# Layer 2's input products in the fixed order of steps, with the latents in seven products of halves

## The chip, the cores and the metric

The kernel runs on one core of a Trainium2 chip. That core has a matrix engine (TensorE, PE in the profile; its weight loads are listed as PEld), a vector engine (VectorE, DVE), an activation engine (ScalarE, ACT), a general engine (GpSimd, POOL) and a synchronisation engine (SyncE, SP) which here only issues DMAs. Each works through a queue of its own, in order, and the engines wait for each other by semaphores. The metric is the device time of the whole kernel in microseconds (us). Three runs of the kernel before took 2256.12, 2256.44 and 2257.72 us; the median is 2256.44.

## What is computed

Two layers on one sequence of 512 tokens of 2048 numbers, everything in fp32. Layer 1 mixes tokens by retention, layer 2 by multi-head latent attention (MLA). Both take an input that is normalised and then shifted and scaled by a vector of modulation, and both multiply their result by a gate.

```python
def mla_branch(h, pos, w_in, q_norm_g, w_uq, kv_norm_g, w_ukv, w_out):
    proj = h @ w_in
    cq, ckv, k_rope, g = jnp.split(
        proj, [MLA_Q_RANK, MLA_Q_RANK + MLA_KV_RANK, MLA_Q_RANK + MLA_KV_RANK + MLA_ROPE], axis=-1)
    q = (rmsnorm(cq, q_norm_g) @ w_uq).reshape(B, S, MLA_HEADS, MLA_NOPE + MLA_ROPE)
    q = jnp.concatenate([q[..., :MLA_NOPE], rope(q[..., MLA_NOPE:], pos)], axis=-1)
    kv = (rmsnorm(ckv, kv_norm_g) @ w_ukv).reshape(B, S, MLA_HEADS, MLA_NOPE + MLA_V)
    k_rope = rope(k_rope[:, :, None, :], pos)
    ...
    return (jax.nn.silu(g) * o) @ w_out

def reference(...):
    c_act = jax.nn.silu(c)
    for i in range(DEPTH):
        mod = (c_act @ ada_w[i] + ada_b[i])[:, None, :]
        shift, scale, gate = jnp.split(mod, 3, axis=-1)
        h = rmsnorm(x, norm_g[i]) * (1.0 + scale) + shift
        ...
        x = x + gate * y
    return rmsnorm(x, final_norm_g)
```

The latents cq and ckv have 512 columns each, the rotary key 64, the gate g 2048, so w_in of layer 2 is 2048 x 3136.

## The kernel before

**Products.** TensorE multiplies in fp32r, which holds fewer digits than fp32. Every operand is therefore split into a high part (a cast, on ScalarE) and a low part (the difference, on VectorE): `split`, lines 131 to 133. A product is three matmuls, high by high, low by high and high by low (`mm3`, lines 156 to 160). A tile is 128 x 128 weights against up to 512 columns. Weights come in units, mostly 256 rows by 512 columns (512 KB): a load on SP's queue, a split, and then 2 x 4 products, 24 matmuls.

**Seven products.** Layer 1's value and gate projections don't use 2 x 2 products of halves but seven products of sums and differences of halves (the scheme of Strassen in Winograd's form): `form_sums` (line 593) forms the sums of the activations, `seven_steps` (line 682) loads weights, forms their sums and runs sixteen steps for each head.

**The list of steps.** Layer 1 is a list `steps`, gone through in one loop (lines 1274 to 1314). Each `Step` has units of weights (load, prepare), matmuls, evacuations, and hooks `beside` them. Loads run three units ahead, the preparation (split) one step ahead. In step i the loop issues loads, prepares step i+1, uses modulation that is ready, runs the step's matmuls, does the additions of the modulation rows fetched before, fetches new rows (`rows` of the next step), and evacuates. The wrappers `behind` and `queued` set the place of instructions in the engines' queues when the program is built; afterwards the order is fixed. `n_p` is the step at which layer 1's pool of buffers is changed and the rotary tables are loaded back.

**Modulation rows.** The later pieces of the modulation come beside other work, a row at a time (`later_modulation`, line 811): SP loads 512 KB of ada_w into one of two buffers (`mod_aw`, line 819), VectorE multiplies it by an element of c and adds it to `mod_am` (line 828). After 16 rows TensorE sums the piece over partitions by matmuls with ones (`sum_modulation`, line 834), and `use_modulation` (line 854) stores it. The last two pieces, 32 rows, are layer 2's gate vector.

**The boundary.** At the end of layer 1, token blocks of 128 are finished one after the other. `x1_out` adds the residual and stores x, `x1_token` (line 1237) scales the block by its norm, in place, on ScalarE (line 1241) and VectorE (line 1242). `h2_pair` (line 1209) transposes two column blocks of x for two token blocks on TensorE into a PSUM bank (x1T, line 1217) and turns them into high and low parts of layer 2's input h2 on ScalarE (lines 1230, 1232) and VectorE (lines 1234, 1235). Banks of that kind come from `aux`, banks for accumulation from `acc`.

**Layer 2 before.** After the list, layer 2 runs by `chunk` and `run`: cq, ckv (`low_rank`, line 1425, 8 units of 24 matmuls each), the rotary keys kr (`kr_unit`, 48 matmuls, each weight column twice), and four gate groups g2 of 8 units of 24 matmuls. A modulation row is fetched with each of the 32 gate units (`next_row`, line 1410). The latents' transposes (cqT, ckvT, line 1449) come in the first group. Then follow the up projections uq and ukv, attention and the output projection.

Of the kernel before, what the change touches and what calls it, by code (L numbers as in the profile page):

```python
# [22 lines left out]
RH = 8  # L23
# [26 lines left out]
def hybrid_trunk_kernel(  # L50
# [219 lines left out]
    def rotary_tables(cos, sin, col, signed, name, queue):  # L270
# [3 lines left out]
        r, k, kh = sin, cos, pos_i.bitcast(F32)  # L274
        DVE.tensor_copy(r, pos_i)
# [179 lines left out]
    tables_d = dram.tile([2 * P, T], F32, name="tables_d")  # L455
# [55 lines left out]
    for u in range(NU):  # L511
# [27 lines left out]
        if more:  # L539
            for k in range(4, KD):  # L540
                queued(add_row, am, aw[k // 2], k, False)
        else:
            for _ in range(7):
                queued(next, tables)
# [38 lines left out]
    sums = {}  # L583

    def sums_tile(n):
# [5 lines left out]
        return lpp.tile(shape, F32R, tag="sums", bufs=4, name=f"sums_{n}")  # L591

    def form_sums(u):
        e, o = (tmp(f"h_{2 * u + i}_f") for i in range(2))
        for f, kt in ((e, 2 * u), (o, 2 * u + 1)):
            DVE.tensor_add(f, hT[kt][:, 0, :].bitcast(F32), hT[kt][:, 1, :].bitcast(F32))
        f = lpp.tile([P, 4, H], F32, tag="own_r", bufs=3, name=f"sums_{u}_f")
        DVE.tensor_add(f[:, 0, :], e[:, H:], o[:, H:])
        DVE.tensor_sub(f[:, 1, :], f[:, 0, :], e[:, :H])
        DVE.tensor_sub(f[:, 2, :], e[:, :H], e[:, H:])  # L600
        DVE.tensor_sub(f[:, 3, :], o[:, :H], f[:, 1, :])
        for i in range(2):
            s = sums_tile(2 * u + i)
            split(f[:, 2 * i : 2 * i + 2, :], s[:, :, 0, :], s[:, :, 1, :])
            sums[2 * u + i] = s

    def form(n, u, b):

        if isinstance(n, tuple):
            kt, half = n  # L610
            o = half * H + b * P
            return tuple(hT[2 * u + kt][:, a, o : o + P] for a in range(2))
# [15 lines left out]
    def plain_steps(nu, kn, parts, cn, name, take, n, lhs, rhs, evac, **kw):  # L628
# [3 lines left out]
        def step(u):  # L632
# [13 lines left out]
            def multiply():  # L646
# [6 lines left out]
                for ki, b in order:  # L653
                    last = u == nu - 1 and ki == kn - 1
                    mm3(banks[b], lhs(w["hl"], ki, u * kn + ki, b), rhs(w["hl"], ki, u * kn + ki, b), u + ki == 0, last)
# [6 lines left out]
            return Step(load, prepare, multiply, follow, **{k: v(u) for k, v in kw.items()})  # L662
# [6 lines left out]
    turn = [0, 0]  # L669

    def raw_tile(shape, name):
        turn[0] += 1
        if turn[0] % 2:
            return base.tile(shape, F32, tag="raw", bufs=3, name=f"{name}_r")
        return lpp.tile(shape, F32, tag="own_r", bufs=3, name=f"{name}_r")

    def part_tiles(shape, name):
        turn[1] += 1
        pool, tags, n = (lpp, ("own_h", "own_l"), 1) if turn[1] % 4 == 0 else (base, ("whi", "wlo"), 3)
        return [pool.tile(shape, F32R, tag=tag, bufs=n, name=f"{name}_{tag[-2]}") for tag in tags]  # L680

    def seven_steps(h):
# [3 lines left out]

        def block(kt, j):
            return wvg[kt * P : (kt + 1) * P, j, h * T : (h + 1) * T]
# [13 lines left out]
        def step(second, u):  # L702
# [54 lines left out]
            def follow():  # L757
# [9 lines left out]
                if second and u == KD // 2 - 1:  # L767
                    for b in range(2):
                        keep_rows(x_[b], v_d, h * T + b * P, f"v{h}_st{b}")
                    for b in range(2):  # L770
                        keep_rows(s_[b], g_d, h * T + b * P, f"g{h}_st{b}", AF.Silu, tmp)
                    for b in range(2):
                        r0 = h * T + (2 + b) * P
                        DVE.tensor_add(m4[b], m4[b], y_[b])
                        POOL.dma_start(v_d[r0 : r0 + P, :], m4[b])
                        DVE.tensor_add(m5[b], m5[b], y_[b])
                        ACT.activation(m5[b], m5[b], AF.Silu)
                        POOL.dma_start(g_d[r0 : r0 + P, :], m5[b])
# [16 lines left out]
    for h in range(1, RH):  # L795
# [9 lines left out]
        steps += seven_steps(h)  # L805
# [356 lines left out]
    wide = [o1_unit(3, 0, u, 1, 2 * T, 2 * (("big", 16),) if u in (4, 5) else (("whi", 3), ("wlo", 3))) for u in range(8)]  # L1162
# [9 lines left out]
    for t in range(NT):  # L1172
# [64 lines left out]
    def x1_token(t):  # L1237
        s1 = small(f"x1_s1_{t}")
        DVE.tensor_reduce(out=s1, in_=ss1[t], axis=AX.X, op=ALU.add)
        r = rsqrt(s1, 1, 1.0 / D, f"x1_{t}")  # L1240
        ACT.activation(x1[t][0], x1[t][0], AF.Identity, scale=r)
        DVE.tensor_scalar(out=x1[t][1], in0=x1[t][1], scalar1=r, scalar2=None, op0=ALU.mult)
        if t == 3:
            h2_pair(0, 8, KD)
            h2_pair(1, 0, KD)


    def all_rows():
# [3 lines left out]
        yield from later_modulation(pools["l1"], [(1, 1, n) for n in range(2)], ("odd1", "odd0"))  # L1252

# [20 lines left out]
    for i, step in enumerate(steps):  # L1274
        clock[0] = i
        if i == n_p:
# [3 lines left out]
            with behind(S_):  # L1280
                for n, name in enumerate(("cos", "sin")):
                    rotary.append(rot(pools["l1"], name))
                    nc.sync.dma_start(rotary[n], tables_d[n * P : (n + 1) * P, :])
        with behind(S_):
            while n_loaded < min(n_prepared + 3, len(loads)):
                loads[n_loaded]()
                n_loaded += 1
            for load in step.beside["load"]:
# [14 lines left out]
        with behind(V_, A_):  # L1303
# [3 lines left out]
            if step.sums is not None:  # L1307
                form_sums(step.sums)
# [429 lines left out]
```

## Time and profile before

| | |
|---|---|
| median of three runs | 2256.44 us |
| profiled execution, its own time | 2255.62 us |
| its span (first to last instruction) | 2253.9 us |
| mean granted clock of TensorE | 0.993 |
| layer 2 from the first x1T (1498.38) to the first uq matmul (1799.86) | 301.48 us |
| HBM read, written | 388.59 MB, 42.48 MB |

The profile is one execution, recorded on the chip. A page lists each engine's busy time, the chain of waits that ended last (followed back from the last instruction), the costliest groups of instructions and the DMA issues. A group is given by its line in the kernel, its engine and operation, output <- inputs with the names of the program, tile shapes and count, then busy time in us, mean length of one in ns, and the idle time of that engine just before, with what ended it. A line of a timeline begins with the start and the length in us; in brackets is the idle time before it and its cause. Matmuls overlap: the distance between their starts, not their length, is what one costs.

### The profile page before, as it was taken

How to read it: one execution, taken by the hardware profiler on the slowest of the kernel's cores; microseconds unless marked ns; L12 is line 12 of the kernel's file. 1: busy time of each engine (PE TensorE's matmuls, PEld its weight loads, DVE VectorE, ACT ScalarE, POOL GpSimd, SP SyncE). 2: the span in 40 equal slices, each digit the busy share in tenths (PEclk: the TensorE clock that was granted, in tenths of full speed). 3: DMA queues.
4: the chain of work that ended last, by engine and by line, in shares of the span. 5: the costliest groups of instructions: out<-in, count | busy, mean ns of one | idle time of the engine just before them, and what ended most of it. 6: DMA issues, size and time to landing. Idle time of an engine off the chain costs nothing.

```text
span 2253.9 us, 27801 instructions
## 1 busy us (share of the span) xinstructions
PE 2193.4 (97%) x10198; PEld 1819.2 (81%) x10198; DVE 1528.9 (68%) x2272; ACT 988.6 (44%) x1488; POOL 113.8 (5%) x205
## 2 busy tenths in 40 slices
PE   5999999999999999999999999999999999999997
PEld 4887888888888888878888888878888888888886
DVE  7988867776676789656777767455454367777545
ACT  5664433434343444434445445444322255555433
POOL 1000000100000000000000000010000000000000
PEclk9999999999999999999999999999999999999999
DMA  9974686767767678564655564532466432235433
GB/s 342 347 240 162 197 292 188 265 213 248 239 219 255 217 248 282 196 201 146 209 173 201 168 206 159 188 125 89 133 222 224 152 106 80 85 99 173 150 126 117
DMA packets 236650, 432.94 MB, mean 192 GB/s; under 512 B 21256, under 2 KB 95072, under 8 KB 236512
## 3 DMA queue, kind: packets, MB, share of 16 engines
q1 hardware_dynamic: 223664, 392.49, 53.9%
q0 software_dynamic: 12416, 38.39, 4.3%
q8 instruction: 80, 1.31, 0.2%
q14 instruction: 58, 0.48, 0.1%
q10 hardware_dynamic: 432, 0.27, 0.0%
HBM read 388.59 MB, written 42.48 MB: 191 GB/s over the span
## 4 chain that ended last, share of the span: by engine, by line
PE 76%; issue 10%; DVE 7%; ACT 5%; DMA 1%; POOL 0%; SPq 0%; POOLq 0%; DVEq 0%; ACTq 0%
PE o L1110 12%; PE qk L160 4%; PE qk L159 4%; PE qk L158 4%; PE g L158 3%; PE g L159 3%; PE g L160 3%; PE o L158 2%; PE o L160 2%; PE o L159 2%; PE x L694 2%; PE y L695 2%; PE x L695 2%; PE y L693 2%; PE y L694 2%
## 5 line engine op out<-in xcount | busy, mean ns | idle before, releaser
L1110 PE MATMUL o<-o_whi,o_h 128*128 128x512 f32 x496 | 194.7, 393 | 0.0
L1110 PE MATMUL o<-o_wlo,o_h 128*128 128x512 f32 x496 | 193.7, 391 | 0.0
L1110 PE MATMUL o<-o_whi,o_l 128*128 128x512 f32 x496 | 193.6, 390 | 0.0
L158 PE MATMUL qk<-hT,qk_h 128*128 128x512 f32 x448 | 176.8, 395 | 3.4 <-ACT qk_h L132 3.4
L160 PE MATMUL qk<-hT,qk_l 128*128 128x512 f32 x448 | 176.3, 393 | 1.0 <-DVE qk_l L133 1.0
L159 PE MATMUL qk<-hT,qk_h 128*128 128x512 f32 x448 | 175.4, 392 | 0.0
L828 DVE SCALAR_TENSOR_TENSOR mod_am<-mod_aw,cact,mod_am 128x1024 f32<-128x1024 f32 x120 | 153.5, 1279 | 11.4 <-DMA mod_aw<-in_ada_w_dram 11.0
L133 DVE TENSOR_TENSOR o_wlo<-o_r,o_whi 128x1024 fp32r<-128x1024 f32 x62 | 75.7, 1223 | 87.8 <-ACT o_whi L132 87.7
L1110 PEld LDWEIGHTS o<-o_whi,o_l 128*128 128x128 f32 x496 | 93.5, 189 | 19.6
L133 DVE TENSOR_TENSOR qk_l<-qk_r,qk_h 128x1024 fp32r<-128x1024 f32 x56 | 68.1, 1222 | 60.2 <-ACT qk_h L132 59.7
L1110 PEld LDWEIGHTS o<-o_wlo,o_h 128*128 128x128 f32 x496 | 93.5, 188 | 19.0
L1110 PEld LDWEIGHTS o<-o_whi,o_h 128*128 128x128 f32 x496 | 93.5, 189 | 19.0
L158 PEld LDWEIGHTS qk<-hT,qk_h 128*128 128x128 f32 x448 | 84.9, 189 | 21.7 <-ACT qk_h L132 4.1
L158 PE MATMUL g<-h,g_hi 128*128 128x512 f32 x256 | 100.6, 393 | 1.1 <-ACT ckv_n L1435 1.1
L160 PEld LDWEIGHTS qk<-hT,qk_l 128*128 128x128 f32 x448 | 84.8, 189 | 20.6 <-DVE qk_l L133 3.0
L158 PE MATMUL o<-o_w_hi,o_h 128*128 128x512 f32 x256 | 100.1, 391 | 0.0
L159 PE MATMUL o<-o_w_lo,o_h 128*128 128x512 f32 x256 | 99.8, 390 | 0.0
L159 PE MATMUL g<-h,g_hi 128*128 128x512 f32 x256 | 99.6, 389 | 0.0
L160 PE MATMUL g<-h,g_lo 128*128 128x512 f32 x256 | 99.6, 389 | 0.0
L160 PE MATMUL o<-o_w_hi,o_l 128*128 128x512 f32 x256 | 99.6, 390 | 0.0
L159 PEld LDWEIGHTS qk<-hT,qk_h 128*128 128x128 f32 x448 | 84.8, 189 | 18.1 <-issue 0.5
L132 ACT CAST qk_h<-qk_r 128x1024 fp32r<-128x1024 f32 x56 | 57.9, 1049 | 88.5 <-PE qk L159 63.5
(1358 smaller groups left out, 5763.0 us busy)
## 6 DMA issues: line engine op xcount, KB each, us to landing
mod_aw<-in_ada_w_dram SPq DMA_DIRECT2D x128, 512.0 KB, 5.2
aw<-in_ada_w_dram SPq DMA_DIRECT2D x128, 256.0 KB, 6.0
o_r<-in_ret_w_out_dram SPq DMA_DIRECT2D x64, 512.0 KB, 4.4
qk_r<-in_ret_w_in_dram SPq DMA_DIRECT2D x112, 256.0 KB, 3.9
g_raw<-in_mla_w_in_dram SPq DMA_DIRECT2D x32, 512.0 KB, 3.7
o_w_raw<-in_mla_w_out_dram SPq DMA_DIRECT2D x32, 512.0 KB, 3.7
qk_d<-qk_st POOLq DMA_DIRECT2D x32, 256.0 KB, 3.9
qk_r<-qk_d SPq DMA_DIRECT2D x32, 256.0 KB, 6.2
```

The lines of the kernel that those rows point to most:

```text
L132: ACT.copy(hi, src)
L133: DVE.tensor_sub(lo, src, hi.bitcast(F32))
L158: PE.matmul(o, lhs[0], rhs[0], start=first and not seeded, stop=False, skip_group_check=seeded)
L159: PE.matmul(o, lhs[0], rhs[1], start=False, stop=False, skip_group_check=seeded)
L160: return PE.matmul(o, lhs[1], rhs[0], start=False, stop=last, skip_group_check=seeded)
L693: PE.matmul(banks[b], a[0], w[0], start=first, stop=False, skip_group_check=True)
L694: PE.matmul(banks[b], a[0], w[1], start=False, stop=False, skip_group_check=True)
L695: PE.matmul(banks[b], a[1], w[0], start=False, stop=True, skip_group_check=True)
L828: DVE.scalar_tensor_tensor(out=am, in0=aw, scalar=ck, in1=am, op0=ALU.mult, op1=ALU.add)
L1110: PE.matmul(o, a[i], w[j][:, ki, cols], start=first and i + j == 0, stop=last and i == 1, skip_group_check=True)
```

## The change

1. Layer 2's input products become steps of the list: five steps `front`, the rest of gate group 0 (`ga`), gate group 1 (`g1`), the latents, gate groups 2 and 3 (`g23`). The loop opens layer 2's pool at the first of them (`n_l2`).
2. cq and ckv are computed together by seven products, with the two latents as the two halves of the columns: 16 steps, 336 matmuls of 512 columns in place of 384. `form_sums` forms the sums of h2 beside steps of gate groups 0 and 1.
3. The rotary key's weights lie high and low part side by side in 128 columns. Two passes, with h2's high and low part, make 64 matmuls of 256 columns in place of 48 of 512; then the two halves of the result are added (`kr_sum`) and the rotation follows (`kr_rope`).
4. The first three units of gate group 0 and the rotary keys are multiplied for the first 256 tokens (`ga_half(u, 0)`, `kr_half(0)`), then for the others. The second half of h2 is transposed beside them. In the last token's step, pairs 0 and 1 of the first half are transposed during its matmuls, pairs 2 and 3 before token 3's scaling, pairs 4 to 7 behind it (`last_token`).
5. The rotary tables of MLA are computed beside the last steps of layer 1, stored, and loaded back at `n_l2`.
6. The 32 rows of layer 2's gate vector are fetched in `g23` only: one in each of the first four steps, two in each of the other twelve; what remains is fetched behind the last step.
7. In layer 1, rows are taken in all steps of the second phases from head 5 on (before: head 6), sums of modulation run in the last head's second phase, and at `n_p` the loads of weights stand ahead of those of the tables. One unit of the output projection's weights goes to another buffer.

The core of the diff, with removed parts of layer 2 (`low_rank`, `kr_unit`, the four groups, `next_row`) left out where only their place changes:

```diff
-            return Step(load, prepare, multiply, follow, rows=int(second and (u % 2 == 1 or (h > 5 and u > 0))))
...
+            lambda second, u: int(second and (u % 2 == 1 or (h > 4 and u > 0))),
+            lambda second, u: second and h == RH - 1 and 2 < u < 7,
...
-        step.follow = lambda t=t: (x1_out(0, t), x1_out(1, t), x1_token(t))
+        step.follow = lambda t=t: (x1_out(0, t), x1_out(1, t), x1_scale(t, x1_factor(t)))
...
         if (t, r) == (3, 1):
-            queued(h2_pair, 0, 0, 8)
+            queued(h2_pair, 0, 0, 4)
...
-        if t == 3:
-            h2_pair(0, 8, KD)
-            h2_pair(1, 0, KD)
-
+    def last_token():
+        x1_out(0, 3)
+        x1_out(1, 3)
+        r = x1_factor(3)
+        h2_pair(0, 4, 8)
+        x1_scale(3, r)
+        h2_pair(0, 8, KD)
+
+    steps[-1].follow = last_token
...
+    def ga_half(u, th):
...
+        cols = slice(th * H, (th + 1) * H)
+        hi, lo = ga[u].w["hl"]
+        for ki in range(2):
+            for b in range(4):
+                o = ga[0].banks[b][:, cols]
+                for i, (w, a) in enumerate(((hi, 0), (hi, 1), (lo, 0))):
+                    PE.matmul(
+                        o, w[:, ki, b * P : (b + 1) * P], h2[2 * u + ki][:, a, cols],
+                        start=u + th + ki + i == 0, stop=False, skip_group_check=True,
+                    )
...
+    def kr_half(th):
+        cols = slice(th * H, (th + 1) * H)
+        if th == 0:
+            kr["ps"] = aux("kr_ps")
+        for kt in range(KD):
+            for a in range(2):
+                PE.matmul(
+                    kr["ps"][:, cols], kr["w"][kt // 8][:, kt % 8].rearrange("p j n -> p (j n)"), h2[kt][:, a, cols],
+                    start=kt + a == 0, stop=kt == KD - 1 and a == 1, skip_group_check=True,
+                )
...
+    front[0].multiply = lambda: (ga_half(0, 0), ga_half(1, 0), queued(h2_pair, 1, 0, 4))
+    front[1].multiply = lambda: (ga_half(2, 0), kr_half(0), queued(h2_pair, 1, 4, 8))
+    front[2].multiply = lambda: (ga_half(0, 1), ga_half(1, 1), queued(h2_pair, 1, 8, 12))
+    front[3].multiply = lambda: (ga_half(2, 1), ga[3].multiply(), queued(h2_pair, 1, 12, KD))
+    front[4].multiply = lambda: (ga[4].multiply(), kr_half(1))
+    steps += front + ga[5:]
+    ga[5].beside["form"].append(kr_sum)
+    ga[6].beside["form"].append(kr_rope)
+    g1 = g2_steps(1)
+    steps += g1
...
+    for u, step in enumerate((ga[5], ga[7], g1[0], g1[2], g1[3], g1[5], g1[6], g1[7])):
+        step.beside["form"].append(lambda u=u: form_sums(u, h2, sums2, staged2, more2))
...
+    steps += seven_steps(
+        "c", lambda kt, j: wc[kt * P : (kt + 1) * P, j, :], lambda n, u, b: form(h2, sums2, n, u, b), *turns2,
+        latent_rows, lambda second, u: 0, lambda second, u: False,
+    )
+    g23 = g2_steps(2, rows=lambda u: 1 if u < 4 else 2) + g2_steps(3, rows=lambda u: 2)
+    for i, n, g_c in ((0, "q", qn_c), (1, "kv", kvn_c)):
+        g23[i].beside["form"].append(lambda n=n: latent_norm(n))
+        g23[i + 1].beside["form"].append(lambda n=n: latent_scale(n))
+        g23[2 + 2 * i].beside["multiply"].append(lambda n=n: latent_transposes(n))
+        g23[3 + 2 * i].beside["form"].append(lambda n=n, g_c=g_c: latent_parts(n, g_c))
+    for step in g23[8:]:
+        step.banks_free = True
+    steps += g23
...
+        yield from later_modulation(pools["l2"], [(1, 2, n) for n in range(2)])
...
+        if i == n_l2:
+            assert not ripe and not summed
+            l1.__exit__(None, None, None)
+            l2 = tc.tile_pool(name="l2", bufs=1)
+            pools["l2"] = l2.__enter__()
         with behind(S_):
             while n_loaded < min(n_prepared + 3, len(loads)):
                 loads[n_loaded]()
                 n_loaded += 1
+            if i in (n_p, n_l2):
...
-    assert next(later, None) is None and not fetched and not ripe and not summed
-    l1.__exit__(None, None, None)
+    for adds in (fetched, later):
+        for add in adds:
+            add()
+    sum_modulation(0)
+    use_modulation()
```

More of the change, by code (lines that the diff above doesn't have):

```diff
@@ new lines, in hybrid_trunk_kernel, with next_tables @@
+    steps[-1].follow = last_token
+    mla_tables = []
+    def next_tables():
+        if not mla_tables:
+            pair = [rot(pools["l1"], f"mla_{n}") for n in ("cos", "sin")]
+            mla_tables.extend((rotary_tables(*pair, 1, True, "mla", nc.sync), pair))
+        if next(mla_tables[0], 0) == 0:
+            for n, t in enumerate(mla_tables[1]):
+                POOL.dma_start(tables_d[(2 + n) * P : (3 + n) * P, :], t)
+    for i in range(10):
+        steps[n_p + 65 + i].beside["form"].append(next_tables)
```

341 lines of the change are left out of this document (180 added, 161 removed).

## The prediction

> **What bounds the kernel now.** I read the page first: busy shares, the chain of waits, the costliest groups and the DMA issues.
>
> ```profile
> span 2253.9 us, 27801 instructions
> PE 2193.4 (97%) x10198; PEld 1819.2 (81%) x10198; DVE 1528.9 (68%) x2272; ACT 988.6 (44%) x1488; POOL 113.8 (5%) x205
> PE 76%; issue 10%; DVE 7%; ACT 5%; DMA 1%; POOL 0%; SPq 0%; POOLq 0%; DVEq 0%; ACTq 0%
> L158 PE MATMUL qk<-hT,qk_h 128*128 128x512 f32 x448 | 176.8, 395 | 3.4 <-ACT qk_h L132 3.4
> L160 PE MATMUL qk<-hT,qk_l 128*128 128x512 f32 x448 | 176.3, 393 | 1.0 <-DVE qk_l L133 1.0
> L828 DVE SCALAR_TENSOR_TENSOR mod_am<-mod_aw,cact,mod_am 128x1024 f32<-128x1024 f32 x120 | 153.5, 1279 | 11.4 <-DMA mod_aw<-in_ada_w_dram 11.0
> L158 PE MATMUL g<-h,g_hi 128*128 128x512 f32 x256 | 100.6, 393 | 1.1 <-ACT ckv_n L1435 1.1
> mod_aw<-in_ada_w_dram SPq DMA_DIRECT2D x128, 512.0 KB, 5.2
> ```
>
> TensorE is busy 97% of the span and carries most of the chain, so a matmul less is its issue time less, and a stall of TensorE is a stall of the end. The last two columns of a group show where TensorE still waits: 3.4 and 1.0 us on retention weights, 1.1 us before the first gate group of layer 2.
>
> Then I cut layer 2's stretch before attention into stages. Columns: window, length, busy time and instructions by engine, granted clock, DMA share, GB/s.
>
> ```profile
> 1498.38:1562.80 64.42, 58.68 (x269) 46.16 (x268) 35.93 (x68) 36.56 (x69) 3.35 (x6) 0.95 0.28 85
> 1562.80:1606.50 43.70, 43.70 (x194) 35.96 (x192) 20.54 (x33) 15.28 (x26) 2.48 (x5) 1.00 0.39 117
> 1606.50:1617.38 10.88, 10.88 (x49) 8.96 (x48) 4.46 (x5) 2.71 (x5) 0.92 (x2) 1.00 0.45 147
> 1617.38:1636.81 19.43, 18.37 (x89) 15.24 (x88) 14.11 (x17) 9.74 (x15) 0.55 (x1) 1.00 0.50 151
> 1636.81:1709.29 72.48, 72.48 (x329) 60.31 (x328) 38.56 (x36) 20.21 (x25) 4.05 (x8) 1.00 0.68 219
> 1813.46:1819.21 5.75, 5.75 (x49) 5.74 (x48) 3.35 (x5) 3.19 (x6) 0.00 (x0) 1.00 0.32 94
> ```
>
> The first window is the boundary (layer 1's last token, the transposes of x, then cq), the second ckv, the third the rotary keys, the fourth the transposes of cq and the first three gate units. The key window is 48 matmuls of 512 columns in 10.88 us: 0.2267 us each (their listed 0.39 us overlap). The ckv window gives the same, 192 in 43.70. The last row is 48 matmuls of 256 columns in 5.75 us: 0.120 each, a little over half.
>
> ```profile
> 1498.38 1.47 PE L1217 MATMUL x1T<-ident,x 128*128 128x128 f32 x12
> 1499.61 0.71 PE L1110 MATMUL o<-o_big,o_h 128*128 128x512 f32 x2
> ```
>
> Twelve transposes go out in the 1.23 us between these two rows of TensorE's timeline, 0.10 each. So the boundary's work is 12 output matmuls, 192 of cq and 64 transposes: 2.7 + 43.5 + 6.4 = 52.6 us. It takes 64.42, so about 11.8 us are stall (and slower clock: 0.95 granted).
>
> **The arithmetic.** Latents: 384 matmuls of 512 columns become 336, −48 × 0.2267 = −10.9 us. Keys: 48 × 0.2267 = 10.9 become 64 × 0.120 = 7.7, −3.2. Three gate units on halves: 72 × 0.2267 = 16.3 become 144 × 0.120 = 17.3, +1.0. Sum −13.1 us. All of it is on the path, as TensorE has no other cover.
>
> **Retention weights.** The waits of 3.4 and 1.0 us are one place, the change of pools at layer 1's seventh q/k unit. In the changed order weight loads stand ahead of the rotary-table loads on SP's queue there, and layer 1's modulation rows have been summed earlier. I take −4.4; bounds −4.4 and 0.
>
> **The keys' tail.** In the fourth window 73 matmuls and 16 transposes need 16.5 + 1.6 = 18.1 of 19.43 us. The new order puts the latents' transposes a whole step after their scaling, so −1.3; bounds −1.3 and 0.
>
> **The boundary.** What governs it is ScalarE and VectorE, which turn transposed x into h2 pair by pair:
>
> ```profile
> 1501.67 1.15 ACT L1241 ACTIVATE x<-x,x_r 128x1024 f32<-128x1024 f32 x1 [3.63 <-DMA x_d<-x]
> 1502.73 0.54 ACT L1230 ACTIVATE h<-x1T,b_col,a_col 128x256 fp32r<-128x256 f32 x1
> 1513.42 0.69 DVE L1084 TENSOR_TENSOR x<-o_g,o_xr 128x512 f32<-128x512 f32 x1
> 1519.32 1.15 ACT L1241 ACTIVATE x<-x,x_r 128x1024 f32<-128x1024 f32 x1 [2.17 <-DMA x_d<-x]
> 1524.86 0.61 ACT L1232 ACTIVATE h2f<-x1T,b_col,a_col 128x256 f32<-128x256 f32 x1
> 1526.21 0.63 ACT L1232 ACTIVATE h2f<-x1T,b_col,a_col 128x256 f32<-128x256 f32 x1
> 1510.00:1530.00 20.00, 15.84 (x70) 11.90 (x70) 15.70 (x33) 15.02 (x33) 1.69 (x3) 0.83 0.25 79
> ```
>
> ScalarE takes 1.35 us a pair (1524.86 to 1526.21). Twice it stands in its queue behind the scaling of x, which waits until x has been stored: the last sum on VectorE ends at 1514.11, the scaling starts at 1519.32, 5.2 us later. The units on half the tokens are there so that TensorE can start when tokens 0 and 1 are ready. But queues run in order, and I read the changed order engine by engine. On TensorE all eight transposes of the first half stand ahead of the first half-token matmul, and each from the third on waits for a bank that VectorE and ScalarE have to empty. On VectorE the two sums of token 3, four instructions, stand between pairs 2 and 3, and on ScalarE token 3's scaling, with its wait for the store, stands between pairs 4 and 5. From the first transpose: pair 1 at +4.3 us (1502.73, that wait is unchanged), two pairs to about +7, the four VectorE instructions to +10, the store to +15.1, the scaling 1.15, then pairs 5 to 7 with their VectorE halves to about +22.4. Until then TensorE has 12 output matmuls and 32 transposes, 5.9 us; it idles 16.5, and 0.8 more later, where ScalarE's 11 us for the other half's pairs meet 12.5 us of half-token and key matmuls. That is 17.3 against 11.8: +5.5. Bounds: −10 (the wait for the store alone decides, and every other stall goes) and +8 (the 0.83 clock lasts 15 us longer, 0.17 × 15 on top).
>
> [...]
>
> **Start of the seven products.** Their first accumulations need the banks of gate group 1, which ScalarE must empty, with the split of the first weights in the same queues. In the trace of before no layer-2 row shows it; the gate group's wait of 1.1 us in the page is nearest. The seven-product form opens with two sets of banks instead of one, so I take +2; bounds 0 and 4.
>
> **Work put beside the gate steps.** Eight sums of h2 add on VectorE, by sizes, about 4.4 us each (two of 512 elements, four of 256, two split differences): 35 us; ScalarE's copies less. They lie beside 16 gate steps of 5.44 us. In before's gate window VectorE is busy 38.56 of 72.48 us with a modulation row per unit, and those rows are gone from there, so they cost nothing; uncovered they would cost those 35 us. The tables' stores (POOL) and reloads (SP) are four transfers of 256 KB in low-traffic stretches: nothing.
>
> **The modulation rows.** This is the term that decides. Before, 32 rows of 512 KB are spread over 32 units. After, they come only in gate groups 2 and 3: one a step for four steps, two a step for twelve, four left for after the last step. Each is a load into one of two buffers and a VectorE addition; a load is issued only when its buffer's addition is done. What such a pair takes is in before's trace, in places where two rows came together with a gate load:
>
> ```profile
> 1651.65 2.60 DVE L828 SCALAR_TENSOR_TENSOR mod_am<-mod_aw,cact,mod_am 128x1024 f32<-128x1024 f32 x2
> 1657.62 1.28 DVE L828 SCALAR_TENSOR_TENSOR mod_am<-mod_aw,cact,mod_am 128x1024 f32<-128x1024 f32 x1 [0.44 <-DMA mod_aw<-in_ada_w_dram]
> ...
> 1652.95 1.66 SPq L819 DMA_DIRECT2D mod_aw<-in_ada_w_dram  x2
> ...
> 1740.46 2.60 DVE L828 SCALAR_TENSOR_TENSOR mod_am<-mod_aw,cact,mod_am 128x1024 f32<-128x1024 f32 x2
> 1746.38 1.28 DVE L828 SCALAR_TENSOR_TENSOR mod_am<-mod_aw,cact,mod_am 128x1024 f32<-128x1024 f32 x1 [0.39 <-DMA mod_aw<-in_ada_w_dram]
> ...
> 1653.00:1659.00 6.00, 6.00 (x29) 4.95 (x28) 3.75 (x3) 1.05 (x1) 0.00 (x0) 1.00 0.79 266
> ...
> mod_aw<-in_ada_w_dram SPq DMA_DIRECT2D x28, 512.0 KB, 4.6
> g_raw<-in_mla_w_in_dram SPq DMA_DIRECT2D x27, 512.0 KB, 3.8
> ```
>
> From addition to addition it is 5.97 us (1651.65 to 1657.62), and 5.92 at the second place. It is 1.28 of addition and some 4.65 of load, and VectorE ends up waiting for the DMA. A gate step is 24 × 0.2267 = 5.44 us. So a pair a step does not fit: it runs late by 0.53 us a step, and the four left over have no step at all. Behind a waiting addition stand, in VectorE's queue, the splits of the next weights; in SP's queue, behind a row's load, the loads of gate, uq and ukv weights; in TensorE's queue the two matmuls that sum the last vector stand in the middle of uq, after its first 21 matmuls, with the rest of attention behind.
>
> There are 14 pairs. The first comes in step 5 of the 16, the second stands behind the ckv latents' parts on VectorE, which I place 13.5 us after the start of step 5. From there the rows need 12 × 5.97 + 2.6 + 0.3 = 74.5 us to the last sum. TensorE has left 12 × 5.44 − 13.5 + 16 transposes (1.6) + 21 × 0.2267 (4.8) = 58.2 us. Difference +16.3. Bounds: a load as fast as a gate load (3.8) makes the pair 5.1 us and the term +6; a load of 5.2, the median of all rows in the page, makes it 6.5 and +23.
>
> [...]
>
> **Sum.** −13.1 − 4.4 − 1.3 + 5.5 + 2.0 + 16.3 = +5.0 us on the profiled execution's 2255.62 (its span is 1.7 of that shorter; nothing here changes those): 2260.6. The median of the runs shown is 0.8 above it, 2256.44, so I say 2261; the rivals' times stand on that median too.
>
> **The rivals.**
> 1. Rows keep up (faster). If a row lands like a gate load, 3.8 us, the term is +6 and the sum −5.3: 2251.1; if the boundary's stall does not grow either, −10.8: 2245.6. For: bandwidth is left by the rows above. Against: 5.97 and 5.92 were measured with just these three loads in flight. It decides from a pair of 5.2 us downwards (12 × 5.2 + 2.9 − 58.2 = +7.1, sum −4.2). Chance 0.27; it is the case the bandwidth figure speaks for.
> 2. Traffic piles up (slower). Three loads of 512 KB in each step and the gate stores load the DMA for 65 us without a pause, where before shows 0.79 for 6 us; the pair goes to 6.5 us or over, and the term to +23 and more: sum +11.7, 2268.1. It decides from a load of 5 us upwards. For: the median of 5.2 us over all rows. Against: 4.6 in the gate groups. Chance 0.18.
> 3. No net change. The half-token units fill the boundary as before's cq does, its term is 0, and the sum −0.5: 2255.9. For: the early matmuls exist. Against: they stand behind eight transposes. Chance 0.15.
>
> My forecast keeps 0.40. About 0.2%, 4.5 us, is what a measurement of this kernel tells from no change. The forecast's +5.0 lies just beyond it, so of its 0.40 I give 0.31 to slower and 0.09 to no change; with case 2, slower has 0.49; no change 0.09 + 0.12 from case 3 = 0.21; faster 0.27 + 0.03 = 0.30. The range takes in most of 1, and 2 with the load of 5.2 and 5 us of boundary: 2246 to 2273. The forecast's own is 2257 to 2266.
>
> **What would show it.** In the changed profile: TensorE waiting on DVE for a transpose ahead of the first half-token matmul (boundary), some 17 us between first transpose and there; waits of L160 on weight splits late in gate group 3, and a wait of over 8 us at the last vector's sum inside uq; additions a pair apart by 6 us; the 3.4 us at the retention weights gone. Wrong would be: additions 5.4 us apart or less, no hole in uq, or half-token matmuls within 10 us of the first transpose; or 256-column matmuls far from 0.120 us each.

## The result, and the profile after

| | before | changed |
|---|---|---|
| median | 2255.34 us (22 runs, 2251.9 to 2257.72) | 2251.93 us (22 runs, 2246.94 to 2254.86) |
| profiled execution, span | 2255.62, 2253.9 us | 2254.86, 2253.1 us |

The changed kernel takes 0.9985 of the time of the one before, with a 95% interval of 0.9979 to 0.9992: 3.4 us faster. The forecast was 2261, 5 us slower. The time lies in the range of the prediction, the sign is wrong. The changed kernel's profiled execution is the slowest of its 22 runs, so its profile shows less gain (0.8 us) than the medians.

The page of the changed kernel:

```profile
span 2253.1 us, 28084 instructions
PE 2178.4 (97%) x10238; PEld 1812.8 (80%) x10238; DVE 1601.9 (71%) x2389; ACT 1012.1 (45%) x1526; POOL 113.9 (5%) x201
PE 72%; DVE 12%; DMA 7%; ACT 5%; issue 4%; POOL 0%; SPq 0%; ACTq 0%; DVEq 0%; POOLq 0%
L857 DVE SCALAR_TENSOR_TENSOR mod_am<-mod_aw,cact,mod_am 128x1024 f32<-128x1024 f32 x120 | 153.6, 1280 | 34.9 <-DMA mod_aw<-in_ada_w_dram 34.8
L158 PE MATMUL qk<-hT,qk_h 128*128 128x512 f32 x448 | 175.3, 391 | 0.0
```

TensorE has 15 us less to do, and the wait of 3.4 us at qk is gone. VectorE's waiting for modulation rows has grown from 11.4 to 34.9 us, and the chain that ended last now has 12% of DVE and 7% of DMA, where it had 7% and 1%.

TensorE's waits in the whole of the changed kernel, the main ones (what it waited for; us in total, times, longest):

```profile
PE xT_ps L476 <- ACT x L453: 17.5, 4, 10.5
PE mod_ps L877 <- DVE mod_am L857: 10.7, 1, 10.7
PE x1T L1246 <- DVE h2f L1263: 8.9, 3, 5.7
...
PE uq L160 <- DVE uq_lo L133: 2.4, 1, 2.4
PE x1T L1246 <- DVE o_g L1112: 1.3, 1, 1.3
PE g L160 <- DVE g_l L133: 1.1, 2, 0.6
```

The first is at the start of the program and was 17.3 us before. Of the others the longest are at the two places that the prediction named: the sum of the last modulation vector in uq (10.7 and 2.4 us), and the transposes at the boundary (8.9 and 1.3 us).

The stages of the changed kernel, in the columns used for the kernel before:

```profile
939.00:1000.00 61.00, 61.00 (x278) 50.92 (x277) 32.83 (x42) 21.05 (x28) 6.47 (x12) 1.00 0.69 229
1490.95:1550.84 59.89, 49.66 (x334) 45.12 (x332) 37.34 (x72) 34.16 (x66) 3.37 (x6) 0.89 0.30 95
1550.84:1610.70 59.86, 59.86 (x266) 49.57 (x265) 47.52 (x79) 25.43 (x37) 2.20 (x4) 1.00 0.40 127
1722.00:1780.00 58.00, 57.45 (x249) 46.07 (x248) 37.58 (x34) 14.48 (x20) 5.28 (x10) 1.00 0.79 270
1780.86:1807.44 26.58, 13.48 (x41) 8.99 (x40) 13.89 (x16) 3.88 (x6) 2.08 (x4) 0.68 0.72 241
```

The first is the change of pools in layer 1. The second runs from the first transpose of x to the end of the keys' second half: the boundary. Its work is 12 output matmuls, 64 transposes, 144 + 64 matmuls of 256 columns and 48 of 512: 2.7 + 6.4 + 25.0 + 10.9 = 45.0 us, so 14.9 us are stall. The third, 264 gate matmuls, runs without a gap (264 × 0.2267 = 59.85) although VectorE is busy for 47.52 us of it. The last runs from the first uq to the first uk matmul: 36 matmuls, 8.2 us, and the vector's sums, some 1.3, take 26.58 us.

Layer 2 began at 1490.95 in place of 1498.38 us, 7.4 earlier; its first uk matmul starts at 1807.44, in the kernel before at 1808.02. From the first transpose on, the changed kernel is therefore 6.9 us slower in its profiled execution, 316.49 against 309.64. What it won, it won before layer 2 and in matmuls; what it lost, it lost at the boundary and in uq.

### The profile page after: what moved, and what is told of

Same layout as the page of the kernel before. It is cut to its first block, busy times and chain, and to the rows that moved or that the text cites. A ratio compares the mean times of both kernels' runs of the same rounds, so it can differ in the third digit from the quotient of the medians.

```text
span 2253.1 us, 28084 instructions
## 1 busy us (share of the span) xinstructions
PE 2178.4 (97%) x10238; PEld 1812.8 (80%) x10238; DVE 1601.9 (71%) x2389; ACT 1012.1 (45%) x1526; POOL 113.9 (5%) x201
## 4 chain that ended last, share of the span: by engine, by line
PE 72%; DVE 12%; DMA 7%; ACT 5%; issue 4%; POOL 0%; SPq 0%; ACTq 0%; DVEq 0%; POOLq 0%
PE o L1139 12%; PE qk L160 4%; PE qk L158 4%; PE qk L159 4%; DMA aw<-in_ada_w_dram 2%; DMA mod_aw<-in_ada_w_dram 2%; PE o L158 2%; PE o L160 2%; PE o L159 2%; PE x L696 2%; PE y L696 2%; PE x L697 2%; PE y L697 2%; PE y L695 2%; PE x L695 2%
## 5 line engine op out<-in xcount | busy, mean ns | idle before, releaser
L857 DVE SCALAR_TENSOR_TENSOR mod_am<-mod_aw,cact,mod_am 128x1024 f32<-128x1024 f32 x120 | 153.6, 1280 | 34.9 <-DMA mod_aw<-in_ada_w_dram 34.8
L370 DVE SCALAR_TENSOR_TENSOR am<-aw,cact,am 128x512 f32<-128x512 f32 x118 | 88.7, 752 | 3.6
L160 PE MATMUL g<-h,g_l 128*128 128x512 f32 x232 | 90.6, 391 | 0.6 <-DVE g_l L133 0.6
L158 PE MATMUL g<-h,g_h 128*128 128x512 f32 x232 | 91.0, 392 | 0.0
```

The lines of the kernel that those rows point to most:

```text
L158: PE.matmul(o, lhs[0], rhs[0], start=first and not seeded, stop=False, skip_group_check=seeded)
L160: return PE.matmul(o, lhs[1], rhs[0], start=False, stop=last, skip_group_check=seeded)
L370: DVE.scalar_tensor_tensor(out=am, in0=aw[:, k % 2], scalar=ck, in1=am, op0=ALU.mult, op1=ALU.add)
L857: DVE.scalar_tensor_tensor(out=am, in0=aw, scalar=ck, in1=am, op0=ALU.mult, op1=ALU.add)
```

## The experiments

Times are medians of the runs in question; the ratio is to the kernel before, timed on the same chip. "Against changed" is the difference to 2251.93. The kernel before took 2255.15 to 2255.94 us on these chips (medians), and the intervals reach 2 to 3 us to either side, so a difference of 1 us shows nothing.

| run | what | median us | ratio, 95% interval | against changed |
|---|---|---|---|---|
| e1 | half of the rows go to attention | 2239.44 | 0.9927, 0.9914 to 0.9941 | −12.5 |
| e2 | four row buffers | 2237.27 | 0.9923, 0.9911 to 0.9936 | −14.7 |
| e7 | e2, two rows in every step | 2238.80 | 0.9928, 0.9916 to 0.9940 | −13.1 |
| e5 | latents by plain products | 2262.23 | 1.0028, 1.0016 to 1.0039 | +10.3 |
| e4 | layer 1's edits undone | 2260.25 | 1.0022, 1.0013 to 1.0030 | +8.3 |
| e9 | only the order of loads undone | 2251.65 | 0.9984, 0.9975 to 0.9993 | −0.3 |
| e10 | only the rows and sums undone | 2259.05 | 1.0012, 1.0003 to 1.0021 | +7.1 |
| e8 | no half-token units | 2258.84 | 1.0018, 1.0009 to 1.0027 | +6.9 |
| e3 | half-token units ahead of transposes | 2252.11 | 0.9990, 0.9981 to 0.9999 | +0.2 |
| e12 | token 3's scaling last | 2250.83 | 0.9979, 0.9971 to 0.9988 | −1.1 |
| e13 | e2 and e12 | 2237.34 | 0.9916, 0.9902 to 0.9930 | −14.6 |
| e14 | e2, e12 and e3 | 2240.52 | 0.9932, 0.9918 to 0.9946 | −11.4 |

### The modulation rows: e1, e2, e7

```diff
 e1
-    g23 = g2_steps(2, rows=lambda u: 1 if u < 4 else 2) + g2_steps(3, rows=lambda u: 2)
+    g23 = g2_steps(2, rows=lambda u: 1) + g2_steps(3, rows=lambda u: 1)
...
+            next_row()
             run(uq, 1)
...
             run(uq)
+            next_row()
             next(a0)
             next(a1)
+            next_row()
             run(ukv_chunk(pr + 1, *tiles_[2:]))
```

> The changed kernel with one modulation row in each of the sixteen gate steps instead of two, and the other sixteen rows between the heads of attention. Theory (a pair of rows takes 6.01 us from addition to addition in the changed profile, a gate step 5.44, so the rows end late and TensorE stands 2.4 + 10.7 us in uq and then runs at a lower clock): the hole in uq goes, the first uq to the first uk matmul falls from 26.6 us to about 9, and the whole is 15 to 18 us shorter than the changed kernel, some 2235. Rival (the hole is there for another reason, such as the loads of uq and ukv weights or the splits after a long queue on VectorE): the hole shrinks by less than half and the time stays within 6 us of the changed kernel. Rival two (rows cost the same wherever they lie): attention grows by what uq loses, time as the changed kernel.

The hole is gone. TensorE's timeline, the first uq and the first uk matmul, of e1:

```profile
1778.28 0.39 PE L158 MATMUL uq<-qT,uq_hi 128*128 128x512 f32 x1
...
1786.44 0.39 PE L158 MATMUL uk<-kvT,ukv_hi 128*128 128x512 f32 x1
```

From one to the other it is 8.16 us, which is 36 × 0.2267 with nothing between. From the first transpose to uk it is 295.35 us, 21.1 less than in the changed kernel's profile. In the time only 12.5 us show. Part of the difference is that profile itself, 2.9 us above its median; part is given back: from uk to the end of the span e1 takes 451.3 us, the changed kernel 445.7. The theory held, 2.5 us short of its range; the second rival, that rows cost wherever they lie, holds for some 5.6 us of attention.

```diff
 e2
+                if (i, sect) == (1, 2):
+                    aw = base.tile([P, 2, T], F32, tag="k4b", bufs=4, name=f"{name}_aw{k}")
```

> The changed kernel with four buffers for the modulation rows of layer 2 instead of two; rows are fetched at the same steps and the same bytes move. Theory (the pair's 6 us is waiting for the two buffers: 4.65 us of load after 1.28 us of addition): with loads issued two earlier, rows keep up with the 5.44 us steps, only the four rows left over behind the last step remain, and the time falls by 10 to 15 us against the changed kernel, to about 2238 to 2242. Rival (the DMA's bandwidth, 275 GB/s in this stretch, sets the pair's 6 us): pairs stay 6 us apart, the time within 3 us of the changed kernel.

e2 moves the same bytes in the same steps. It is 14.7 us faster, as the theory had it, so the two buffers were the limit, and not what the DMA can carry in this stretch. The additions in the changed kernel, on VectorE, the second and the last of the pairs, with what they waited for:

```profile
1722.69 2.60 DVE L857 SCALAR_TENSOR_TENSOR mod_am<-mod_aw,cact,mod_am 128x1024 f32<-128x1024 f32 x2
...
1794.78 1.28 DVE L857 SCALAR_TENSOR_TENSOR mod_am<-mod_aw,cact,mod_am 128x1024 f32<-128x1024 f32 x1 [0.26 <-DMA mod_aw<-in_ada_w_dram]
1797.74 1.28 DVE L857 SCALAR_TENSOR_TENSOR mod_am<-mod_aw,cact,mod_am 128x1024 f32<-128x1024 f32 x1 [1.68 <-DMA mod_aw<-in_ada_w_dram]
```

Twelve pairs from 1722.69 to 1794.78: 6.01 us each in the mean. They are not a steady cycle, though: eight of the twelve took 4.7 to 5.8 us, less than a step or little more, and four took 6.9 to 9.1. The longest spans the end of gate group 2, where ScalarE's last evacuation waits for an earlier one to be stored, and the cast of the next weights stands behind it:

```profile
1737.54 0.60 ACT L1310 ACTIVATE sgs<-g 128x512 f32<-128x512 f32 x1 [3.73 <-DMA sg_d<-sgs]
1738.03 1.99 ACT L132 CAST g_h<-g_r 128x1024 fp32r<-128x1024 f32 x2
```

e2 has that wait too, 4.97 us, and still keeps up. The same stretch as in the changed kernel's stages, with four buffers:

```profile
1722.00:1780.00 58.00, 57.09 (x247) 45.91 (x246) 46.32 (x44) 14.06 (x19) 4.72 (x9) 1.00 0.86 305
```

The DMA moves 305 GB/s, where the changed kernel has 270, and the single load takes longer, not shorter (median 5.8 us from issue to landing from 1720 to 1783 us, against 4.3). Nor are the 270 GB/s a ceiling: from 1720 to 1783 us the changed kernel moves up to 419 GB/s in a slice of 1.6 us, loads and stores together.

> The kernel with four row buffers, and two rows in every step of gate groups 2 and 3, so that none of the 32 rows is left behind the last step. Theory (with four buffers the rows' pace is set by the steps and only what lies behind the last step stands in the way; first x1T to first uk matmul is 300.6 us with four buffers, 295.4 where no row holds uq): 4 to 6 us faster than with four buffers alone, some 2232. Rival (the first steps of group 2, where VectorE also turns the latents into their parts, have no room for two rows, and the weights' splits come late): the same time or slower, 2237 to 2240.

In e7 two rows are fetched from the first step of group 2 on, and none is left at the end. It is no faster than e2 (2238.80 and 2237.27), as the rival's time had it: from the first transpose to uk it takes 300.50 us, e2 300.64. The four rows behind the last step cost nothing that shows, once loads run ahead. Most of what e2 takes over e1's 295.35 are the sums of the two vectors on TensorE, some 1.7 us each, which e1 has in attention.

### The matmuls: e5

e5 puts cq and ckv back as two products of eight units each, in the same place of the list, without `form_sums` for h2.

> The changed kernel with the latents as two plain products of 8 units each (384 matmuls of 512 columns) in the same place of the list, and without the sums of h2. Theory (a matmul less is 0.2267 us less, and the sums of h2 lie beside gate steps at no cost): 48 x 0.2267 = 10.9 us slower than the changed kernel, 9 to 12, some 2263. Rival (the sums, some 35 us of VectorE's work, and the weights' sums cost the steps beside them part of the gain): less than 7 us slower.

It is 10.3 us slower than the changed kernel, for 10.9 of matmuls, as the theory had it. The sums of h2 and of weights cost nothing that shows; the intervals would hide 2 us.

### The change of pools in layer 1: e4, e9, e10

```diff
 e4 (both parts); e9 has only the second part, e10 only the first
-            lambda second, u: int(second and (u % 2 == 1 or (h > 4 and u > 0))),
-            lambda second, u: second and h == RH - 1 and 2 < u < 7,
+            lambda second, u: int(second and (u % 2 == 1 or (h > 5 and u > 0))),
+            lambda second, u: False,
...
         if i == n_p:
             ...
+            with behind(S_):
+                for n, name in enumerate(("cos", "sin")):
+                    rotary.append(rot(pools["l1"], f"{name}_0"))
+                    nc.sync.dma_start(rotary[n], tables_d[n * P : (n + 1) * P, :])
         ...
-            if i in (n_p, n_l2):
+            if i == n_l2:
```

> The changed kernel with its edits in layer 1's list undone: rows from head 6 on, the sums of modulation where they were, and the rotary tables' loads ahead of the weights' at the change of pools. The prediction priced these edits at 4.4 us, the sum of the waits listed. Theory (the listed waits are followed by a stretch at a lower clock, 0.69 in 960 to 965 us, so the place cost about 7 us): this kernel is 6 to 8 us slower than the changed one. Rival (only the listed waits): 4 to 5 us slower. Rival two (the earlier start of layer 2, 1490.95 against 1498.38 us, comes from elsewhere): within 2 us.

8.3 us slower, a little over what the theory of waits and clock gave. The window at the place, in the kernel before, and then its parts:

```profile
939.00:1000.00 61.00, 57.09 (x261) 47.28 (x260) 29.00 (x39) 16.50 (x23) 4.79 (x9) 0.94 0.60 203
...
954.92:958.41 3.49, 3.49 (x34) 3.49 (x32) 0.00 (x0) 0.00 (x0) 0.00 (x0) 1.00 0.00 0
958.41:963.04 4.63, 4.63 (x15) 3.66 (x15) 0.00 (x0) 0.00 (x0) 0.00 (x0) 0.64 0.64 192
963.04:965.79 2.75, 2.75 (x12) 1.91 (x10) 0.38 (x1) 0.00 (x0) 0.00 (x0) 0.99 0.96 333
965.79:969.17 3.38, 0.00 (x0) 0.00 (x0) 2.41 (x5) 1.56 (x2) 0.00 (x0) 1.00 1.07 369
969.17:973.48 4.31, 3.78 (x10) 2.72 (x11) 3.59 (x5) 1.14 (x2) 0.00 (x0) 0.60 0.51 153
```

The changed kernel has 61.00 busy at 1.00 (above). Here the listed waits are 3.4 and 0.5 us, from 965.79 on, and TensorE is slow twice: for 4.63 us *ahead* of the wait, at a granted clock of 0.64, and for 4.31 us behind it, at 0.60. Each costs some 1.7 us, so the place costs 3.9 + 1.7 + 1.7 = 7.3 us, and layer 2 began 7.4 us earlier without it. (The expectation of e4 takes the slow stretch of 960 to 965 us for one behind the wait; it lies ahead of it.) In e4 the wait is 3.7 us, and the slow stretches are at 0.59 for 4.20 us and 0.52 for 6.82 us.

The first slow stretch begins right behind 32 matmuls of one column in a row, the sums of modulation (954.92 to 958.41). It is there in all three traces that have 32 in a row: this one, e4, and e10 (0.51 for 3.10 us). The changed kernel has them in two groups of 16 (925.19 and 931.12), and its clock is 1.00 from 923 to 937 us. So part of what the earlier sums gain is this, and not the wait; no run tested it alone.

The second slow stretch lies behind the waits, 3.4 and 0.5 us here: from 971.02 to 973.16 us matmuls start 0.428 us apart in place of 0.227. That the length of the wait decides is not shown: e10 has the same stretch (0.60 for 4.31 us) behind waits of 2.0 and 0.5 us.

> The changed kernel with one of the two edits at the change of pools undone: the rotary tables' loads stand again ahead of the weights' loads; rows and sums of modulation stay as changed. Both edits undone gave +8.3 us. Theory (SP waits at the tables' loads for the freed pool, and the weights behind come late): 6 to 8 us slower than the changed kernel. Rival (the rows and the sums, which keep the pool in use, are the cause): within 2 us.

> The changed kernel with the other edit at the change of pools undone: rows from head 6 on and sums of modulation as before, while the weights' loads stay ahead of the rotary tables' loads. Undoing the order of the loads alone gave nothing (2251.65), undoing both +8.3 us. Theory (the sums of modulation, which use the old pool until after its change, hold whatever SP issues into the new one; with the weights ahead of the tables only the tables wait): within 2 us of the changed kernel, either edit being enough. Rival (the late sums themselves hold TensorE or the weights, whatever the order of the loads): 3 to 8 us slower, and the rows are the whole cause.

The order of the loads, which the prediction gave as the first cause, is worth nothing once the sums come early (e9, as its rival had it). The rows and the sums, undone together, are the cause (e10, 7.1 of the 8.3 us); e10's theory that either edit is enough was wrong. SP's queue at the loads of the tables shows where the wait comes from, first in the kernel before, then in the changed one:

```profile
958.62 0.34 SPq L1283 DMA_DIRECT2D cos<-tables_d  x1
959.01 0.43 SPq L1283 DMA_DIRECT2D sin<-tables_d  x1
959.55 0.90 SPq L638 DMA_DIRECT2D qk_r<-in_ret_w_in_dram  x2
```

```profile
951.91 0.34 SPq L1518 DMA_DIRECT2D cos<-tables_d  x1
952.31 0.72 SPq L1518 DMA_DIRECT2D sin<-tables_d  x1
953.08 1.19 SPq L922 DMA_DIRECT2D qk_r<-qk_d  x2
```

And TensorE's timeline in the kernel before:

```profile
954.92 3.63 PE L841 MATMUL mod_ps<-ones,mod_am 128*128 128x1 f32 x32
```

The tables go into buffers of the new pool, so they wait until the sums of modulation have read the old one: the 32 sums end at 958.55, the table's load is issued at 958.62. All weights behind it come late. In e10 one more unit of weights stands ahead of the tables, which are issued at 958.66; the wait shrinks from 3.7 us (e4) to 2.0, but does not go. With the sums a few steps earlier the tables are issued at 951.91, and TensorE has no wait here.

### The boundary: e8, e3, e12

In e8 the first three gate units run on all 512 tokens, each behind a quarter of the second half's transposes, and both halves of the keys after unit 4.

> The changed kernel without the half-token units: each of the first three gate units on all 512 tokens, behind the transposes of a quarter of the second half each, and the keys' two halves together behind unit 4. TensorE has 1.0 us less of matmuls. Theory (the half-token and key matmuls are what TensorE has while ScalarE takes 11 us for the second half's pairs): 6 to 11 us slower than the changed kernel. Rival (they gain nothing, as ScalarE's pairs set the boundary anyway): within 3 us of the changed kernel.

6.9 us slower, as the theory had it. From the first transpose to the first matmul of the seven products it takes 127.53 us, the changed kernel 119.75; and this with fewer matmuls. TensorE's first waits are the changed kernel's (5.8, 0.2, 1.3 and 3.0 us), and further ones of 1.8, 0.3 and 3.5 us follow, ahead of the second half's transposes and of the first gate unit, which wait for VectorE and ScalarE. So the half-token units do fill the later part of the boundary, beside the pairs on ScalarE, where the prediction had set them.

```diff
 e3
         x1_scale(3, r)
-        h2_pair(0, 8, KD)
...
-    front[0].multiply = lambda: (ga_half(0, 0), ga_half(1, 0), queued(h2_pair, 1, 0, 4))
+    front[0].multiply = lambda: (
+        ga_half(0, 0), queued(h2_pair, 0, 8, 12), ga_half(1, 0), queued(h2_pair, 0, 12, KD), queued(h2_pair, 1, 0, 4),
+    )
```

> The changed kernel with the last four transposes of the first half placed behind the first half-token gate unit and the second one on TensorE's queue, instead of all ahead of both. Theory (the transposes, which wait for banks that ScalarE empties after token 3's scaling, keep the half-token matmuls from filling the hole): the 5.8 us of these matmuls go into the 10.1 us of idle time, and the time falls by 3 to 5 us. Rival (the pairs of h2 on ScalarE and VectorE set the end of the boundary whatever TensorE does meanwhile): the hole moves behind the early matmuls, the time within 1.5 us of the changed kernel.

The rival held: 2252.11. TensorE's timeline in e3, with the waits:

```profile
1498.04 1.11 PE L1246 MATMUL x1T<-ident,x 128*128 128x128 f32 x4 [5.68 <-DVE h2f L1263]
1498.81 0.78 PE L1333 MATMUL g<-h,g_h 128*128 128x256 f32 x2
...
1512.22 0.66 PE L1246 MATMUL x1T<-ident,x 128*128 128x128 f32 x4 [3.86 <-DVE h2f L1263]
```

The first half-token matmul comes 10.7 us after the first transpose (1488.15) in place of 19.6. But the transposes behind wait longer instead: 5.68 + 3.86 + 0.61 = 10.15 us in all, where the changed kernel has 5.74 + 0.15 + 1.27 + 2.97 = 10.13. To the first matmul of the seven products it takes 119.81 us, the same as 119.75.

```diff
 e12
-        x1_scale(3, r)
         h2_pair(0, 8, KD)
+        x1_scale(3, r)
```

> The changed kernel with token 3's scaling behind all pairs of the first half instead of between pairs 3 and 4 of the eight; nothing else moves. Theory (on ScalarE the scaling's wait for the store of x holds pairs 4 to 7 of the first half, which don't need token 3): the last hole of 3.0 us ahead of a transpose goes, the first half-token matmul comes 2 to 4 us earlier, the time falls by 1 to 4 us. Rival (the second half's pairs, which need the scaling, set the end of the boundary): within 1 us of the changed kernel, the hole moves to the second half.

The time is 1.1 us lower, which the intervals don't tell from nothing, and from the first transpose to the seven products it takes 119.96 us, no less than before the edit. The edit did not take the hole away, nor did the hole move: TensorE's waits are 5.89, 0.16, 1.28 and 2.97 us, and the first half-token matmul comes 19.73 us after the first transpose, against 19.58. Only ScalarE's part of the scaling moved (to 1510.81); VectorE's part kept its place (1504.32), ahead of the h2f that the last transposes wait for. So ScalarE's scaling, with its wait for the store, was not what held these transposes, and e12 doesn't show what their hole is worth.

The largest wait of the boundary, 5.7 to 5.9 us in the traces of the changed kernel and of all the runs, was touched by no run. It is for the first pair's bank, and ScalarE comes to that pair late. In the changed kernel:

```profile
1496.71 1.15 ACT L1272 ACTIVATE x<-x,x_r 128x1024 f32<-128x1024 f32 x1 [2.39 <-DMA x_d<-x]
1497.77 1.03 ACT L132 CAST g_h<-g_r 128x1024 fp32r<-128x1024 f32 x1
1498.70 0.56 ACT L1259 ACTIVATE h<-x1T,b_col,a_col 128x256 fp32r<-128x256 f32 x1
...
1500.90 1.11 PE L1246 MATMUL x1T<-ident,x 128*128 128x128 f32 x4 [5.74 <-DVE h2f L1263]
```

The first pair starts 7.75 us after the first transpose, in the kernel before 4.35 (1502.73): token 2's scaling starts 5.76 us after it in place of 3.29, and a cast of gate weights stands between.

### The gains together: e13, e14

> The two changes that helped, together: four buffers for layer 2's modulation rows and token 3's scaling behind the first half's pairs. Theory (the boundary and the rows are separate places, so the gains add: 14.7 and 1.1 us against the changed kernel's 2251.9): some 2236. Rival (what the boundary saves is lost in the later wait for rows or banks): 2237 to 2239, as four buffers alone.

> The same with the last four transposes of the first half behind the first half-token units as well, and token 3's scaling behind them. Theory (early half-token matmuls were worth nothing while the scaling stood ahead of pairs 4 to 7; with the scaling last they can fill the hole): 2 to 4 us faster than the other kernel of this pair. Rival (the pairs on ScalarE and VectorE set the end of the boundary whatever stands where on TensorE): within 1.5 us of it.

e13 is e2 again (2237.34 and 2237.27), as its rival had it. e14 is 3.2 us slower than e13, with 121.53 us from the first transpose to the seven products in place of 119.71, so there both theory and rival missed. e2, 0.9923 of the time of the kernel before (0.9911 to 0.9936), needs the fewest edits and is the best version found; the intervals don't tell e1, e7 and e13 from it.

## Why the prediction was wrong

**Bound and arithmetic: right.** TensorE's time was what counted. −10.9 us for the latents was measured as 10.3 (e5), and the keys' matmuls of 256 columns took 0.120 us each (32 in 3.83 us). The keys and the half-token units were not tested alone.

**Retention weights: the step that failed.** The prediction put −4.4 us, the listed waits, and gave that as the bound too. The place was worth 8.3 us (e4), and layer 2 began 7.4 us earlier. Waits were priced by their length alone, though the boundary's own row, quoted in the prediction, showed a clock of 0.83 around waits. At the place itself the trace of before has 3.9 us of waits (the page's 1.0 us is two waits, one of them elsewhere) and 3.4 us lost to a clock of 0.64 and 0.60, half of it ahead of the wait. One of the two causes given was wrong too: the order of loads plays no part with the sums early (e9).

**Keys' tail: right.** From 1550 to 1790 us TensorE has no listed wait at the latents' transposes.

**Boundary: mechanism partly right, mis-sized.** The transposes do stand ahead of the half-token matmuls and wait for VectorE. The first such matmul came after 19.6 us, not 22.4, and the stall is 14.9 us against 11.8, +3.1 in place of +5.5; 10.1 us of it are listed waits, the rest is mostly a clock of 0.50 from 1500.90 to 1510.53, which the prediction had only in its bound. That 19.6 is near 22.4 is in part luck, as two errors offset each other: ScalarE's first pair starts 7.75 us after the first transpose and not 4.3, and token 3's scaling with its store (4.4 us where 5.2 was taken) does not stand in the way of the half-token matmuls at all (e12). That the order on TensorE decides was wrong: in e3 the half-token matmuls come 9 us earlier, and nothing is gained. What sets the end instead stays open: the late first pair, VectorE's work for token 3 and the second half's pairs are left, and no run tested them alone. The third rival, that the half-token units fill the boundary as cq did, is about as near as the forecast: +3.1 lies between its 0 and +5.5.

**Start of the seven products: +2.0 was nothing.** TensorE's list of waits has none there; the 1.1 us that it was taken from is a wait for the norm of ckv.

**Side work: right.** Eight sums of h2 cost nothing that shows (e5, and the gapless window above).

**Modulation rows: right in mechanism, and in size partly by luck.** A pair took 6.01 us in the mean against 5.97 predicted, but four long pairs make that mean, and not a steady cycle. The hole in uq costs 26.58 − 8.2 − 1.3 = 17.1 us where +16.3 was predicted. Only 13.1 of the 17.1 are waits (10.7 and 2.4); the other 4.0 are mostly a clock of 0.50 behind them (1799.17 to 1805.30), which the prediction had not counted. The other seven kernels with two buffers and the rows in the same steps have 13.7 to 16.0 there, and e2's time gives 14.7. e2 shows that the waiting for two buffers is the cause. The first rival's time, 2251.1, is met by the measured 2251.93, but by chance: the rows did not keep up, and a pair did not take its 5.1 us. The bandwidth figure that its chance of 0.27 is given for is shown by no run; the runs show 270 GB/s from 1722 to 1780 us, and 305 with four buffers (e2).

**The sum, with the measured terms:** −13.1 − 8.3 − 1.3 + 3.1 + 0 + 17.1 = −2.5 us (−4.9 with e2's 14.7 for the rows), against −3.4 in the medians. The sign turned on the term of the retention weights (3.9 us off), with the boundary (2.4) and the start of the seven products (2.0) off the same way. A forecast of +5.0 whose smaller terms carried errors of 2 to 4 us each was not clear of no change.

## What to carry to other kernels

Price a stall of the bounding engine by its length and by the clock around it: here listed waits of 3.9 us stood in a place worth 7 to 8. A stream that is moved into fewer steps has to be checked against its own pace with the buffers it has, not against the bandwidth: with two buffers a pair took 6.0 us in the mean where the step had 5.44, and two more buffers turned a gain of 3 us into one of 18. When a pool changes, ask what still reads the old one: here the first load into the new one held all of SP's queue until 958.62. And an edit that is meant to remove a wait should be looked up in its trace: e12's wait was still there.

## What the runs showed of the hardware

With four row buffers instead of two the single load took longer (median 5.8 against 4.3 us) and yet the DMA moved more (305 against 270 GB/s from 1722 to 1780 us). Behind 32 matmuls of one column in a row, 3.5 us, the granted clock was 0.51 to 0.64 for 3 to 5 us, in three traces (the kernel before 0.64, e4 0.59, e10 0.51); behind 16 in a row, from 923 to 937 us of the changed kernel, it stayed at 1.00. After the hole of 10.7 us in uq the granted clock is 0.50 for 6.13 us, and the sums of a vector take 2.8 us before the next matmul starts, where e2 has 1.3:

```profile
1799.17 3.75 PE L877 MATMUL mod_ps<-mod_am,ones 128*128 128x512 f32 x4 [10.70 <-DVE mod_am L857]
1801.94 1.42 PE L158 MATMUL uq<-qT,uq_hi 128*128 128x512 f32 x1
```
